# One filling block of a decoder layer moved from the RWKV-7 part to the HGRN2 stage, with the late half projections in other turns and the attention operands in fixed slots

## The chip, the cores and the metric

The kernel runs on one core of one Trainium2 chip. The metric is the device time of one execution in microseconds (us); lower is better. The kernel before took 1496.69 us, the median of three runs (1495.39 to 1498.95).

## The reference, cut to what matters

One decoder layer over 1024 tokens of width 1024, in float32. Three groups of heads work side by side on one input projection; a gated feed-forward with a short convolution, a gated embedding and a last normalization follow.

```
z = rmsnorm(h, norm_mix_g) @ w_in                  # 1024 x 3840
a_q, a_f, a_i, a_g, b_q, b_k, b_v, c_in = split(z)
o_a = hgrn2_mix(a_q, a_f, a_i, a_g, ...)           # 4 heads of 128, gated linear recurrence
o_b = dilated_window_mix(b_q, b_k, b_v)            # 4 heads of 64, three dilated windows
o_c = rwkv7_mix(c_in, ...)                         # 4 heads of 64, delta-rule recurrence
h = h + concat(o_a, o_b, o_c) @ w_out
h = h + conv_glu_ffn(rmsnorm(h), ...)
h = h + sigmoid(rmsnorm(h) @ w_g) * (p @ w_p)
return rmsnorm(h)
```

Sequence 1024, d_ff 2816. The change touches only how and when columns of `z` are computed and how the first two lines of heads use them; what is computed stays.

## The kernel before, in words

**Tiling.** All data lies transposed, channels on the 128 partitions and tokens along the free axis. `w_in` is cut into 30 column blocks of 128. A block is projected by 48 TensorE products of 128x128 by 128x512 (`mm3`, L125-L134): 8 row blocks, 2 halves of the tokens, and 3 products each, since every float32 operand is split into a high and a low part (`xh`, `xl` for the input, `whi`, `wlo` for the weights; `split2`, L102-L109, makes the weights' parts with a ScalarE cast and a subtraction on GpSimd or VectorE). Weights come through two buffers (`wraw`), the split parts through six of each kind (three blocks' worth).

**Stages.** First the norm of the input (`mix_norm`). Then RWKV (`rwkv`): blocks 0 to 7 are its own columns, done in two parts p = 0, 1 of two heads each. In each part there is a preparation, a small triangular inverse that runs on VectorE, and a main part (`rwkv_main`, `rwkv_groups`) of four groups of chunks, a chain of small products on TensorE with VectorE, ScalarE and GpSimd steps between them. The other 22 blocks (8 to 23 for HGRN2, 24 to 29 for attention) don't depend on RWKV, and are used as filling: while RWKV's chain waits for other engines, TensorE computes projections. A list in `rwkv` (L523) fixes their order, and `FILL = (6, 4, 6, 3)` says how many go to part 0's preparation, part 0's main part, part 1's preparation and part 1's main part. In a main part the filling is a generator of steps (`project_steps`): one step is three products, a block has 16, and `fill(k)` calls in `rwkv_groups` place k of them at given points: 11 in a group where the main part has four blocks (`more` = 1), 8 where it has three. A finished block is scaled, sometimes put through a sigmoid, and stored to device memory as `z` by the SP queue (`project_done`, L455).

**The HGRN2 stage** (`phase_mix`, L308-L328) starts when RWKV is through. Three blocks are then still missing. Four streams are interleaved in rounds by a string of letters: A is heads 0 and 2 of HGRN2, B heads 1 and 3 (from round 6), C the attention (`swa`, turns in `TURNS`), F the missing blocks (`project_late`, tiles `zp`), half a block (24 products) a turn, in rounds 1, 3, 5, 7, 9, 11, 13; its last turn frees the projection's input and makes the operand tiles of the output projection in its place. A turn of A or B is one step of a head (`hgrn_head`): load f and q of a head from `z` (SP queue, `zload`), make keys (`hk`) and gated queries (`qt`), scores (`hsc`), seven levels of a hierarchical product (`hsc` at L1023, with multiplications of `qt` and `hk` between them), transposes (`vt`), chunk states (`hkv`), outputs (`hpo`), their norm (VectorE, a power on GpSimd, VectorE), and a last transpose (`vt` at L1106) with the gate. Attention does two pairs of heads, eight query blocks each: scores (`swq`), a VectorE minimum, a ScalarE exponential, transposes (`swt`), values (`swo`). Its operands q, k, v and the turned V share four buffers of one tag, and the next pair's three are loaded together on GpSimd's queue after the last block of the first pair.

The letters give the priority only. A scheduler then writes each engine's instructions in the order in which its model expects them to become ready; each engine executes its list strictly in that order. In the main parts of RWKV the order is the program's own (`manual_schedule`).

**Pools.** Memory pools that are opened with `self.pool` wait for each tile's last user when memory is used again; those of `tc.tile_pool` (`hg`, `sw`, `rk0`, `rk1` before the change) wait for the whole pool.

After the stage `phase_out` multiplies by `w_out` (tiles `dp`), with the operands in the order 6, 7, 0, 1, 4, 2, 3, 5; its first products can fill the end of the HGRN2 stage.

Of the kernel before, what the change touches and what calls it, by code (L numbers as in the profile page):

```python
# [10 lines left out]
F32 = mybir.dt.float32  # L11
# [68 lines left out]
class Trunk:  # L80
# [227 lines left out]
    def phase_mix(self):  # L308
        nc, tc = self.nc, self.tc
        self.mix_norm()  # L310
        with tc.tile_pool(name="slots", bufs=1) as slots:
            self.slots, self.NSLOT = slots, 8
            self.rwkv()
        self.O, self.done = None, []
        for p in (0, 1):
            self.o_split(6 + p)
        with tc.tile_pool(name="hg", bufs=1) as slots, tc.tile_pool(name="sw", bufs=1) as sp:
            self.slots, self.NSLOT = slots, 11
            self.hgrn_setup()
            self.sp = sp  # L320
            self.swmask = sp.tile([P, T], F32, name="swmask")
            nc.scalar.dma_start(self.swmask, self.a["swm"])
            A = chain(self.hgrn_head(0), self.hgrn_head(2))
            B = chain(self.hgrn_head(1), self.hgrn_head(3))
            order = []
            for r in range(36):
                order += "C" * (r in self.TURNS) + "A" + "B" * (r > 5) + "F" * (r % 2 and r < 14)
            interleave(order, {"A": A, "B": B, "C": self.swa(sp), "F": self.project_late(self.rest)})  # L328

    TURNS = [i * 33 // 22 for i in range(23)]  # L330

    def mix_norm(self):

# [182 lines left out]
    def rwkv(self):  # L516
        nc, tc = self.nc, self.tc
        lt = self.mix_in(0, 6, "lora")
        nc.scalar.activation(lt[0:64, :], lt[0:64, :], AF.Tanh)
        sg = self.mix_in(1, 7, "sg")  # L520
        nc.scalar.activation(sg, sg, AF.Sigmoid)
        self.z = {}
        js = iter((*range(8, 16), 24, 25, 26, 16, 17, 18, 20, 21, 22, 27, 28, 29, 19, 23))  # L523
        for p in (0, 1):
            d = {}
            with tc.tile_pool(name=f"pre{p}", bufs=1) as tp:
                with tc.manual_schedule(engines={mybir.EngineType.PE}):
                    self.rwkv_prep(p, tp, lt, d, next(js))
                self.rwkv_inverse(p, tp, d)
            self.project_rest([next(js) for _ in range(self.FILL[2 * p] - 1)])  # L530
            E = mybir.EngineType
            self.pend = {}
            steps = self.project_steps([next(js) for _ in range(self.FILL[2 * p + 1])])
            with tc.tile_pool(name=f"rk{p}", bufs=1) as rp:
                with tc.manual_schedule(engines={E.PE, E.DVE, E.Activation, E.Pool}):
                    self.rwkv_main(p, rp, sg, d, steps)
                    for _ in range(2):
                        next(steps, None)
                    self.pending("w")
                    self.rwkv_norm_out(p, sg, d, 0)  # L540
            self.rwkv_norm_in(p, d, 1)
            for n in steps:
                self.pending("z")
            self.pending("z")
            self.rwkv_norm_out(p, sg, d, 1)
        self.rest = list(js)

    FILL = (6, 4, 6, 3)

    def rwkv_prep(self, p, tp, lt, d, j):  # L550

# [159 lines left out]
    def rwkv_main(self, p, rp, sg, d, steps):  # L711
        y = d["scf"]
        y3 = y.rearrange("p (c v) -> p c v", v=64)
        d.update(y=y, y3=y3)
        self.rwkv_groups(p, rp, d, y3, steps, 11 if self.FILL[2 * p + 1] > 3 else 8)

    def rwkv_norm_in(self, p, d, hf, parts=(0, 1, 2, 3)):

# [43 lines left out]
        if name in self.dbg:  # L762
            self.nc.sync.dma_start(self.dbg[name], t)

    def rwkv_groups(self, p, rp, d, y3, steps, n):

        nc, mxp = self.nc, self.mxp
        ar, v, gC = d["ar"], d["v"], d["gC"]
# [61 lines left out]
        quad("U", 0)  # L830
        nc.vector.memset(X, 0.0)
        nc.vector.memset(GM, 0.0)
        packed_rb(0)
        nc.gpsimd.memset(RB, 0.0)
        nc.gpsimd.memset(Kt, 0.0)
        for q in Q:
            for u in range(4):
                nc.vector.tensor_copy(add[q, u, 1, :], self.ident[q, q])
        add_ar(0)
        S, more = None, 1 if n > 8 else 0  # L840
        for g in range(4):
            cs, last = group(g), g == 3
            c2 = lambda b: slice(4 * g + 2 * b, 4 * g + 2 * b + 2)
# [104 lines left out]
            fill(more)  # L948


    def hgrn_setup(self):
# [19 lines left out]
    def hgrn_head(self, h):  # L971
# [127 lines left out]
        o3 = o.rearrange("p (c v) -> p c v", v=P)  # L1099
        nc.vector.tensor_tensor(o3, o3, rs.unsqueeze(2).broadcast_to([P, 8, P]), ALU.mult)  # L1100
        yield
        for hf in (0, 1):
            sl = slice((1 - hf) * HT, (2 - hf) * HT)
            pt = mxp.tile([P, HT], F32, tag="mx", name=self.nm("vt"))
            for c in range(4):
                nc.tensor.transpose(pt[:, c * P:(c + 1) * P], o3[:, hf * 4 + c, :], self.ident)  # L1106
            nc.vector.scalar_tensor_tensor(oa[:, sl], pt if hf else pt[:, ::-1], par[:, PC_GN + h:PC_GN + h + 1], oa[:, sl], ALU.mult, ALU.mult)
# [4 lines left out]

    def swa(self, sp):

        pend, fin, load = [], None, self.swa_load(sp, 0)
        yield
        for p in (0, 1):
            d = load
            self.swa_values_in(d)
# [17 lines left out]
    def swa_load(self, sp, p):  # L1137
        d = {"p": p}
        for i, n in enumerate("qkv"):
            d[n] = self.zload(24 + 3 * p + i, lambda n: sp.tile([P, T], F32, tag="sslot", name=self.nm(n), bufs=4),  # L1140
                              self.nc.gpsimd)
        return d

    def swa_values_in(self, d):
        nc, vc = self.nc, d["v"]
        V = self.sp.tile([P, T], F32, tag="sslot", name=self.nm("sV"), bufs=4)
# [706 lines left out]
```

## Time and profile before

| | us |
|---|---|
| median of three runs | 1496.69 |
| the profiled execution's own time | 1496.24 |
| its span, first to last instruction | 1494.5 |
| TensorE (PE) busy in the span | 1445.1 (97%) |
| VectorE (DVE) | 1097.8 (73%) |
| ScalarE (ACT) | 634.5 (42%) |
| GpSimd (POOL) | 446.6 (30%) |

In the trace, RWKV's first main part runs from 146.4 to 225.7 us, the second from about 349 to 421.6, and the HGRN2 stage from 433 to about 648. A view by windows gives the busy time of each engine within stretches of the span, and the clock that TensorE was granted (1.00 is full speed). A view of waits adds up, for an engine, the idle time in front of its instructions by what ended it. A timeline row has the start in us, the time from the first start to the last end of the merged instructions, engine, line, operation, tiles, and in brackets the idle time before it with its releaser. Products overlap in the array, so the distance between starts, not the length of one, is what a product costs. A float32 product stands twice in a row's count.

### The profile page before, as it was taken

The numbers are of one execution on the slowest core, as the hardware profiler recorded it, in microseconds if no ns is written. First come the engines' busy times: TensorE is split into PE (matmuls) and PEld (weight loads), VectorE is DVE, ScalarE is ACT, GpSimd is POOL, SyncE is SP. The second block draws the span as 40 slices with busy tenths as digits, with TensorE's granted clock in tenths as the row PEclk, the third lists the DMA queues.
The fourth block names the chain that finished last, engine by engine and source line by source line (L and its number), as shares of the span: only waits on it lengthen the run. The fifth ranks groups of instructions, "written<-read, shape, count | busy, mean of one in ns | idle before, by whom it ended". The sixth has DMA issues, their size and how long they took to land.

```text
span 1494.5 us, 20176 instructions
## 1 busy us (share of the span) xinstructions
PE 1445.1 (97%) x7416; PEld 1199.0 (80%) x7416; DVE 1097.8 (73%) x1650; ACT 634.5 (42%) x1121; POOL 446.6 (30%) x362
## 2 busy tenths in 40 slices
PE   8999999999989889999999999999999999999996
PEld 7888997888977677778878888888888888888775
DVE  7666455585648668736788888888888799777684
ACT  6531343213425635425454444444444444455542
POOL 3232432313412122112144554444554000002343
PEclk9999999999999989999999999999999999999998
DMA  6123112232152111165333333333332883351443
GB/s 219 58 92 99 43 56 72 72 99 63 43 179 74 42 73 57 43 229 194 127 110 98 103 106 106 106 106 106 106 106 81 313 298 97 105 164 42 139 157 106
DMA packets 79874, 167.83 MB, mean 112 GB/s; under 512 B 20064, under 2 KB 22240, under 8 KB 79776
## 3 DMA queue, kind: packets, MB, share of 16 engines
q1 hardware_dynamic: 65424, 145.44, 29.8%
q10 hardware_dynamic: 13264, 17.04, 3.4%
q0 software_dynamic: 1088, 4.06, 0.8%
q8 instruction: 58, 0.95, 0.3%
q14 instruction: 40, 0.33, 0.1%
HBM read 120.12 MB, written 46.40 MB: 111 GB/s over the span
## 4 chain that ended last, share of the span: by engine, by line
PE 84%; DVE 6%; issue 4%; POOL 2%; DMA 2%; ACT 1%; DVEq 0%; POOLq 0%; ACTq 0%; SPq 0%
PE bg L1325 16%; PE bv L1325 12%; PE dp L130 8%; PE dp L134 8%; PE dp L132 8%; PE bg L1626 7%; PE bv L1626 7%; PE hsc L1023 2%; DMA zl<-z 1%; PE swq L1167 1%; PE swo L1203 1%; POOL wlo L108 1%; PE bv L130 1%; PE bv L132 1%; PE swt L1190 1%
## 5 line engine op out<-in xcount | busy, mean ns | idle before, releaser
L130 PE MATMUL dp<-xh,whi 128*128 128x512 f32 x560 | 202.7, 406 | 1.1 <-ACT xh L374 1.1
L134 PE MATMUL dp<-xh,wlo 128*128 128x512 f32 x560 | 194.4, 391 | 2.0 <-POOL wlo L108 1.1
L132 PE MATMUL dp<-xl,whi 128*128 128x512 f32 x560 | 194.5, 391 | 0.4 <-DVE xl L375 0.3
L108 POOL TENSOR_TENSOR wlo<-raw,whi 128x512 fp32r<-128x512 f32 x84 | 138.0, 1662 | 77.8 <-ACT whi L106 77.8
L108 POOL TENSOR_TENSOR wlo<-wraw,whi 128x512 fp32r<-128x512 f32 x64 | 88.0, 1379 | 233.2 <-ACT whi L106 203.9
L1325 PE MATMUL bg<-t,whi 128*128 128x512 f32 x352 | 132.7, 389 | 0.0
L106 ACT CAST whi<-wraw 128x512 fp32r<-128x512 f32 x120 | 72.1, 617 | 132.7 <-PE dp L132 94.4
L134 PEld LDWEIGHTS dp<-xh,wlo 128*128 128x128 f32 x560 | 105.0, 188 | 25.0 <-POOL wlo L108 1.5
L130 PEld LDWEIGHTS dp<-xh,whi 128*128 128x128 f32 x560 | 104.5, 188 | 23.6 <-issue 3.8
L132 PEld LDWEIGHTS dp<-xl,whi 128*128 128x128 f32 x560 | 105.2, 188 | 21.8 <-DVE xl L375 1.4
L108 POOL TENSOR_TENSOR wlo<-s,whi 128x512 fp32r<-128x512 f32 x44 | 65.9, 1498 | 159.5 <-ACT whi L106 147.3
L1626 PE MATMUL bg<-t,whi 128*128 128x512 f32 x308 | 95.0, 389 | 0.0
L1626 PE MATMUL bv<-t,whi 128*128 128x512 f32 x308 | 94.8, 389 | 0.0
L106 ACT CAST whi<-raw 128x512 fp32r<-128x512 f32 x88 | 52.6, 619 | 97.4 <-PE bv L1325 49.0
L106 ACT CAST whi<-s 128x512 fp32r<-128x512 f32 x66 | 38.9, 620 | 120.7 <-PE bg L1325 113.3
L1325 PEld LDWEIGHTS bg<-t,whi 128*128 128x128 f32 x352 | 66.0, 188 | 13.6
L175 POOL TENSOR_TENSOR rst<-rst,mhalf 128x4 f32<-128x4 f32 (+1 forms) x9 | 9.8, 1088 | 223.4 <-DVE rst L173 223.4
L108 DVE TENSOR_TENSOR wlo<-wraw,whi 128x512 fp32r<-128x512 f32 x56 | 48.2, 863 | 34.8 <-ACT whi L106 32.4
L1622 ACT CAST t<-t 128x512 fp32r<-128x512 f32 x77 | 47.8, 622 | 47.8 <-PE bv L1626 34.8
L1626 PEld LDWEIGHTS bv<-t,whi 128*128 128x128 f32 x308 | 57.8, 188 | 12.1
L1626 PEld LDWEIGHTS bg<-t,whi 128*128 128x128 f32 x308 | 57.7, 188 | 12.0
L1325 PE MATMUL bg<-t,wlo 128*128 128x512 f32 x176 | 67.2, 389 | 0.0
(429 smaller groups left out, 3660.9 us busy)
## 6 DMA issues: line engine op xcount, KB each, us to landing
raw<-in_ffn_up_dram SPq DMA_DIRECT2D x44, 512.0 KB, 3.7
wraw<-in_w_in_dram SPq DMA_DIRECT2D x29, 512.0 KB, 3.6
z<-zst SPq DMA_DIRECT2D x19, 512.0 KB, 2.9
gb<-ct SPq DMA_DIRECT2D x33, 256.0 KB, 2.0
t<-gb SPq DMA_DIRECT2D x33, 256.0 KB, 2.8
t<-gt SPq DMA_DIRECT2D x33, 256.0 KB, 2.7
zl<-z SPq DMA_DIRECT2D x16, 512.0 KB, 3.5
wraw<-in_ple_gate_dram SPq DMA_DIRECT2D x16, 512.0 KB, 3.6
```

The costliest lines, as they stand in the source:

```text
L106: nc.scalar.copy(hi, src)
L108: eng.tensor_tensor(lo, src, hi.bitcast(F32), ALU.subtract)
L130: nc.tensor.matmul(ps[hf], wh, xh[hf], start=first, stop=False)
L132: nc.tensor.matmul(ps[hf], wh, xl[hf], start=False, stop=False)
L134: nc.tensor.matmul(ps[hf], wl, xh[hf], start=False, stop=last)
L1023: nc.tensor.matmul(sc[:, c, :], ks[:, c * P:(c + 1) * P], view(qt, c * P, [2 * n, 64 // n], [HT + n, 2], [1, n]), start=True, stop=True)
L1167: nc.tensor.matmul(pq[h][:, b:b + w], d["q"][hs, qb * P:nk], d["k"][hs, b:b + w], start=True, stop=True)
L1190: nc.tensor.transpose(pt[:, kb * P:(kb + 1) * P], lg[:, b + kb * P:b + (kb + 1) * P], self.ident)
L1203: nc.tensor.matmul(po[hs, :], d["V"][:, kb, hs], pT[h][:, kb * P:(kb + 1) * P], start=kb == 0, stop=kb == qb)
L1325: nc.tensor.matmul(ps, w[part == 2][:, s], X[k][part == 1], start=start and k == part == 0, stop=k == 3 and part == 2, skip_group_check=no ...
L1622: nc.scalar.copy(xh, x)
L1626: nc.tensor.matmul(ps[m], wt[part == 2][:, m * P:(m + 1) * P], (xh, xl)[part == 1], start=k == part == 0, stop=k == NK - 1 and part == 2)
```

## The change

`FILL` becomes (6, 3, 6, 3): part 0's main part has three filling blocks instead of four, and all later blocks move up by one, so that four blocks (28, 29, 19, 23) and not three (29, 19, 23) are left for the HGRN2 stage. `rwkv_groups` places 8 steps a group in both parts. F has turns in rounds 0, 1, 4, 7, 9, 11, 13, 15 and a last one in 17. A head's last turn comes one round later (a second `yield` before the final transposes). Attention's operands have a tag each; scores of the first block stand before the transposes of V; the next pair's k is loaded after block 5 (into the place of the first pair's v), its q and v after block 7, q on ScalarE's queue. The pools `hg`, `sw` and `rk` are opened with `self.pool`. At the start of `rwkv_groups`, memsets and copies that need no inverse stand before the two operations (`quad`) that read it.

```diff
-        with tc.tile_pool(name="hg", bufs=1) as slots, tc.tile_pool(name="sw", bufs=1) as sp:
+        with self.pool("hg") as slots, self.pool("sw") as sp:
...
-            for r in range(36):
-                order += "C" * (r in self.TURNS) + "A" + "B" * (r > 5) + "F" * (r % 2 and r < 14)
+            for r in range(38):
+                order += "C" * (r in self.TURNS) + "A" + "B" * (r > 5) + "F" * (r in self.LATE)
...
+    LATE = 0, 1, 4, 7, 9, 11, 13, 15, 17
...
-            with tc.tile_pool(name=f"rk{p}", bufs=1) as rp:
+            with self.pool(f"rk{p}") as rp:
...
-    FILL = (6, 4, 6, 3)
+    FILL = (6, 3, 6, 3)
...
-        quad("T", 0)
+        nc.vector.memset(X, 0.0)
+        nc.vector.memset(GM, 0.0)
...
+        quad("T", 0)
+        quad("U", 0)
         add_ar(0)
...
-            fill(1 + more)
+            fill(1)
...
-            fill(more)
...
         nc.vector.tensor_tensor(o3, o3, rs.unsqueeze(2).broadcast_to([P, 8, P]), ALU.mult)
         yield
+        yield
...
+        ds = {0: {"p": 0}, 1: {"p": 1}}
+        for n, tag in zip("qkv", ("sa", "sb", "sc")):
+            self.swa_load(ds[0], n, tag, nc.gpsimd)
...
                     cur = self.swa_scores(sp, d, qb)
+                if qb == p:
+                    self.swa_values_in(d)
...
-                if qb == 7 and p == 0:
-                    load = self.swa_load(sp, 1)
+                if p == 0 and qb == 5:
+                    self.swa_load(ds[1], "k", "sc", nc.gpsimd)
+                if p == 0 and qb == 7:
+                    self.swa_load(ds[1], "q", "sa", nc.scalar)
+                    self.swa_load(ds[1], "v", "sb", nc.gpsimd)
```

In the order of instructions the change shows at three places of the HGRN2 stage. The first is TensorE's list at the start of the stage: `yt` and `pg` end RWKV, `zp` is a late half projection, `swq` and `vt` are attention's first scores and the transposes of its V, `hsc` the first scores of HGRN2's head 0. Before:

```order
L755 MATMUL pg_3672<-sg_474,par 128x512
L1150 MATMUL vt_3705<-cst,zl_3698 128x128 x4
L1150 MATMUL vt_3711<-cst,zl_3698 128x128 x4
L1167 MATMUL swq_3718<-zl_3696,zl_3694 128x128
L1167 MATMUL swq_3719<-zl_3696,zl_3694 128x128
L130 MATMUL zp_3746<-xh_105,whi_3736 128x512
...
L134 MATMUL zp_3746<-xh_119,wlo_3738 128x512
L1167 MATMUL swq_3790<-zl_3696,zl_3694 128x256
L1167 MATMUL swq_3791<-zl_3696,zl_3694 128x256
L1002 MATMUL hsc_3776<-zl_3702,hk_3729 128x128 x4
```

And with the change:

```order
L756 MATMUL pg_3609<-sg_474,par 128x512
L130 MATMUL zp_3653<-xh_105,whi_3643 128x512
...
L134 MATMUL zp_3653<-xh_119,wlo_3649 128x512
L1171 MATMUL swq_3681<-zl_3633,zl_3631 128x128
L1171 MATMUL swq_3682<-zl_3633,zl_3631 128x128
L1154 MATMUL vt_3692<-cst,zl_3635 128x128 x4
L1154 MATMUL vt_3698<-cst,zl_3635 128x128 x4
L130 MATMUL zp_3710<-xh_89,whi_3643 128x512
...
L134 MATMUL zp_3710<-xh_103,wlo_3649 128x512
L1001 MATMUL hsc_3740<-zl_3639,hk_3705 128x128 x4
```

Two halves (48 products) instead of one now stand ahead of the first `hsc`; the scores of attention's second block moved behind it.

The second place is TensorE's list where attention passes from its first pair of heads to its second. `swt` are transposes of the first pair's exponentials; `swq` with the operands `zl_4396,zl_4394` (before) or `zl_4062,zl_4329` (now) are the second pair's first scores; `hpo` are outputs of HGRN2's head 0. Before:

```order
L1190 MATMUL swt_4383<-cst,lg_4211 128x128 x4
L1190 MATMUL swt_4389<-cst,lg_4211 128x128 x3
L1167 MATMUL swq_4629<-zl_4396,zl_4394 128x128
L1167 MATMUL swq_4630<-zl_4396,zl_4394 128x128
L1167 MATMUL swq_4712<-zl_4396,zl_4394 128x256
L1167 MATMUL swq_4713<-zl_4396,zl_4394 128x256
L1086 MATMUL hpo_4401<-hV_4250,hS_3773 128x128
```

With the change:

```order
L1106 MATMUL vt_4504<-cst,ho_4333 128x128 x4
L1022 MATMUL hsc_4514<-qt_3962,ks_4476 128x128 x4
L130 MATMUL zp_4525<-xh_89,whi_4429 128x512
...
L134 MATMUL zp_4525<-xh_103,wlo_4435 128x512
L189 MATMUL swd_4554<-cst,sden_3912 64x128 x8
L1171 MATMUL swq_4565<-zl_4062,zl_4329 128x128
L1171 MATMUL swq_4566<-zl_4062,zl_4329 128x128
```

The second pair's first scores moved from before head 0's outputs to behind them, behind the two last late halves and behind head 0's final transposes (`vt_4504`).

The third place is TensorE's list ahead of head 0's final transposes (`vt` from `ho`), which wait for the norm of the outputs. Before:

```order
L1190 MATMUL swt_4461<-cst,lg_4353 128x128 x4
L1190 MATMUL swt_4467<-cst,lg_4353 128x128 x4
L1023 MATMUL hsc_4483<-qt_4027,ks_4428 128x128 x4
L1106 MATMUL vt_4534<-cst,ho_4400 128x128 x4
L1106 MATMUL vt_4540<-cst,ho_4400 128x128 x4
```

With the change:

```order
L1022 MATMUL hsc_4416<-qt_3962,ks_4361 128x128 x4
L130 MATMUL zp_4439<-xh_105,whi_4429 128x512
...
L134 MATMUL zp_4439<-xh_119,wlo_4435 128x512
L1022 MATMUL hsc_4468<-qt_3962,ks_4424 128x128 x4
L1207 MATMUL swo_4479<-pT_4380,sV_3691 64x128
...
L1106 MATMUL vt_4498<-cst,ho_4333 128x128 x4
```

A late half, another level of head 1 and 16 products of attention's values moved in between.

More of the change, by code (lines that the diff above doesn't have):

```diff
@@ L714, in rwkv_main @@
         d.update(y=y, y3=y3)
-        self.rwkv_groups(p, rp, d, y3, steps, 11 if self.FILL[2 * p + 1] > 3 else 8)
+        self.rwkv_groups(p, rp, d, y3, steps)
     def rwkv_norm_in(self, p, d, hf, parts=(0, 1, 2, 3)):
@@ L763, in dump, with rwkv_groups @@
             self.nc.sync.dma_start(self.dbg[name], t)
-    def rwkv_groups(self, p, rp, d, y3, steps, n):
+    def rwkv_groups(self, p, rp, d, y3, steps):
         nc, mxp = self.nc, self.mxp
@@ L826, in rwkv_groups @@
         RB5, GM5 = (w.rearrange("p u (a h i) -> p u a h i", a=2, h=2) for w in (RB, GM))
-        quad("T", 0)
+        nc.vector.memset(X, 0.0)
+        nc.vector.memset(GM, 0.0)
+        for q in Q:
+            for u in range(4):
+                nc.vector.tensor_copy(add[q, u, 1, :], self.ident[q, q])
         scores_bd(0)
         keys_bd(0)
-        quad("U", 0)
-        nc.vector.memset(X, 0.0)
-        nc.vector.memset(GM, 0.0)
         packed_rb(0)
@@ L835, in rwkv_groups @@
         nc.gpsimd.memset(Kt, 0.0)
-        for q in Q:
-            for u in range(4):
-                nc.vector.tensor_copy(add[q, u, 1, :], self.ident[q, q])
+        quad("T", 0)
+        quad("U", 0)
         add_ar(0)
-        S, more = None, 1 if n > 8 else 0
+        S = None
         for g in range(4):
@@ L947, in rwkv_groups @@
                     nc.scalar.copy(y4[64 * c:64 * c + 64, 2 * g:2 * g + 2, h, :], py4[64 * h:64 * h + 64, :, c, :])
-            fill(more)
     def hgrn_setup(self):
@@ L1113, in swa @@
     def swa(self, sp):
-        pend, fin, load = [], None, self.swa_load(sp, 0)
+        nc, pend, fin = self.nc, [], None
+        ds = {0: {"p": 0}, 1: {"p": 1}}
+        for n, tag in zip("qkv", ("sa", "sb", "sc")):
+            self.swa_load(ds[0], n, tag, nc.gpsimd)
         yield
         for p in (0, 1):
-            d = load
-            self.swa_values_in(d)
+            d = ds[p]
             for qb in range(10):
@@ L1131, in swa, with swa_load @@
                     pend.append((qb, *cur))
-                if qb == 7 and p == 0:
-                    load = self.swa_load(sp, 1)
+                if p == 0 and qb == 5:
[3 more added lines that the diff above has]
+                    self.swa_load(ds[1], "v", "sb", nc.gpsimd)
                 yield
         self.swa_out(*fin)
[L1137 to L1142, printed above, removed]
+    def swa_load(self, d, n, tag, eng):
+        d[n] = self.zload(24 + 3 * d["p"] + "qkv".index(n),
+                          lambda nm: self.sp.tile([P, T], F32, tag=tag, name=self.nm(nm), bufs=1), eng)
     def swa_values_in(self, d):
         nc, vc = self.nc, d["v"]
-        V = self.sp.tile([P, T], F32, tag="sslot", name=self.nm("sV"), bufs=4)
+        V = self.sp.tile([P, T], F32, tag="sd", name=self.nm("sV"), bufs=1)
         for hf in (0, 1):
```

## The prediction

> **What bounds the kernel now.** I read the page first, then the stages by windows, then what TensorE waits for in the stage that shows gaps.
>
> ```profile
> span 1494.5 us, 20176 instructions
> PE 1445.1 (97%) x7416; PEld 1199.0 (80%) x7416; DVE 1097.8 (73%) x1650; ACT 634.5 (42%) x1121; POOL 446.6 (30%) x362
> PE   8999999999989889999999999999999999999996
> PEclk9999999999999989999999999999999999999998
> ```
>
> TensorE is the bound, 97% busy. The change adds and removes no product worth naming, so it can only win or lose what TensorE loses: idle time and slow clock. The slices show both between the 12th and 18th digit, 410 to 670 us. Windows narrow that down: the two main parts of RWKV, then the whole HGRN2 stage, then the four stretches in it with a clock below 1.00 and those between them.
>
> ```profile
> core 0: us, PE busy (x) PEld busy (x) DVE busy (x) ACT busy (x) POOL busy (x), PEclk, DMA share, GB/s
> 146.40:225.70 79.30, 78.95 (x553) 71.86 (x552) 42.18 (x91) 30.55 (x93) 29.83 (x36) 1.00 0.14 48
> 349.30:421.60 72.30, 70.96 (x513) 64.44 (x512) 41.68 (x89) 29.09 (x91) 28.79 (x35) 1.00 0.15 48
> 433.00:648.00 215.00, 190.43 (x1358) 153.54 (x1357) 150.57 (x289) 105.92 (x208) 46.25 (x39) 0.95 0.21 69
> 445.60:449.00 3.40, 3.40 (x18) 3.40 (x18) 1.95 (x5) 0.40 (x2) 0.21 (x1) 0.50 0.99 314
> 524.10:530.90 6.80, 5.54 (x24) 4.63 (x25) 1.05 (x6) 0.88 (x4) 0.00 (x0) 0.50 0.25 103
> 541.20:548.00 6.80, 5.49 (x34) 5.29 (x36) 5.68 (x8) 1.24 (x2) 1.82 (x3) 0.50 0.01 2
> 575.30:578.70 3.40, 3.37 (x18) 2.74 (x19) 3.30 (x6) 0.27 (x1) 0.00 (x0) 0.50 0.08 14
> ```
>
> RWKV's main parts have almost no gap (0.35 and 1.34 us). The HGRN2 stage has 215.00 - 190.43 = 24.6 us of idle TensorE. In four stretches the clock is half; TensorE is busy there for 3.40 + 5.54 + 5.49 + 3.37 = 17.8 us, which at full speed would be 8.9. So the stage loses 24.6 + 8.9 = 33.5 us. No other engine is near a bound: VectorE is busy 150.57 of 215. What TensorE waits for in the stage, in total, times, longest:
>
> ```profile
> PE vt L1106 <- DVE ho L1100: 8.0, 3, 4.4
> PE swq L1167 <- DMA zl<-z: 5.3, 1, 5.3
> PE hsc L1002 <- DVE hk L984: 3.7, 1, 3.7
> PE hsc L1023 <- DVE qt L1028: 3.4, 4, 1.6
> PE swt L1190 <- ACT ob L1204: 0.9, 1, 0.9
> ```
>
> Three rows hold 17.0 us. Their places in the timeline, with the idle time in brackets:
>
> ```profile
> 445.22 3.41 PE L1002 MATMUL hsc<-zl,hk 128*128 128x128 f32 x16 [3.72 <-DVE hk L984]
> 525.01 0.80 PE L1167 MATMUL swq<-zl,zl 64*128 64x128 f32 x4 [5.31 <-DMA zl<-z]
> 542.51 1.94 PE L1106 MATMUL vt<-cst,ho 128*128 128x128 f32 x8 [4.40 <-DVE ho L1100]
> 644.95 1.06 PE L1106 MATMUL vt<-cst,ho 128*128 128x128 f32 x8 [1.77 <-DVE ho L1100]
> ```
>
> The third wait of that group is 8.0 - 4.40 - 1.77 = 1.8 us, in front of head 1's `vt`. Each of the four slow stretches begins at the end of such a wait (445.6 after 445.22, 524.1 within the one that ends at 525.01, 541.2 within the one to 542.51; the fourth, at 575.3, is at head 1's). The same eight transposes take 1.94 us in the slow stretch and 1.06 outside. So a long wait is paid twice, and the wait of 1.77 that ends at 644.95 brought no slow stretch: the point lies near 1.8 us.
>
> The Trainium skill, TensorE: Matmul & The Clock Gate, section "Part 1: The HAM clock gate (the "warmup" mystery)", says that the array's clock falls to half after an idle window of about 3.4 us and returns after a busy one. The trace agrees with the half and with lengths of 3.40 and 6.80 us. By that rule the stretch after the 1.8 us wait has another cause and stays, 3.37 / 2 = 1.7 us less to win, and the sum below would be 1477.1; the trace puts it right behind a wait, and I follow the trace.
>
> **The change part by part.**
>
> *RWKV's first main part.* The price of a block: a late half is 24 products, and the first and last of one start at
>
> ```profile
> 435.14 0.50 PE L130 MATMUL zp<-xh,whi 128*128 128x512 f32 x1
> 440.48 0.39 PE L134 MATMUL zp<-xh,wlo 128*128 128x512 f32 x1
> ```
>
> so 5.34 / 23 = 0.232 us each, 5.6 a half and 11.1 a block. Part 1 already runs with three blocks and 8 steps a group; it is the row to go by. Part 0 shortens from 79.30 to about 72.30, 7.0 us; four steps fewer remain behind the groups (16 x 4 - 44 - 2 = 18 before, 48 - 32 - 2 = 14 after), 12 products or 2.8 us. That is 9.8 of 11.1: thinner filling costs **+1.3**. Bounds: 0.3 (part 0's gap stays as it is) and 2.6 (twice it). The memsets ahead of `quad` and the pools' finer waits work where TensorE has a gap of 0.35 us in all: nothing to win, and no wait added.
>
> *Start of the stage.* TensorE waits for keys that need head 0's f. SP's queue had been held:
>
> ```profile
> 419.17 15.57 SPq L97 DMA_DIRECT2D wraw<-in_w_out_dram  x2
> 434.80 0.42 SPq L464 DMA_DIRECT2D z<-zst  x1
> 435.38 1.73 SPq L502 DMA_DIRECT2D zl<-z  x2
> 443.04 0.81 DVE L981 TENSOR_SCALAR zl<-zl,olb,lb 128x1024 f32<-128x1024 f32 x1 [6.70 <-DMA zl<-z]
> ```
>
> Two prefetches of `w_out` wait there for weight buffers, then come the last block's store and f's load, which lands 7.7 us later. With the change one prefetch, the store and the loads stand there in the same order, and the prefetch waits for a split that the last filling block's end releases, as now; so I leave f's landing where it is, and the wait is hidden, not shortened: a second half, 5.6 us, stands in front of `hsc`, against 3.72 of wait. **-3.7**. Bounds: 0 (f later by the difference and more) and -3.7. A new wait: GpSimd's load of the next pair's k now waits for both stores of block 28, and behind it in that queue stands head 0's third key multiplication. The second half ends near 446 (440.48 and one half more), its store a few us later, and the multiplication stands now at
>
> ```profile
> 454.90 1.16 POOL L1026 TENSOR_TENSOR hk<-hk,hT 128x512 f32<-128x512 f32 x1
> ```
>
> so I take 0, up to 3 if the store is late.
>
> *The change of pairs.* Before, GpSimd issues the second pair's last loads at
>
> ```profile
> 518.30 1.12 POOL L502 DMA_DIRECT2D zl<-z  x2
> ```
>
> and TensorE's list has the scores that need them ahead of head 0's ready outputs. Now outputs, levels, two halves and the values of two blocks stand between; the two halves alone are 11.1 us, against a landing of 525.01 - 518.30 = 6.7. **-5.3**; it can't cost more than now, and 0 only if the q load were issued over 4.4 us after the first of those halves began. Its issue on ScalarE's queue, some 0.4 us like SP's, is off the path.
>
> *Final transposes of a head.* For head 0 a half (5.6), a level and 16 value products now stand in between, against 4.40; for head 1 a round with two levels and attention. Head 3 is last, has only `dp` products behind it, and keeps its 1.77. **-6.2** (8.0 - 1.8), bounds -8.0 and -3.
>
> *Slow clock.* All four stretches followed waits that go. **-8.9**, bounds 0 and -8.9.
>
> *The added block.* Its 11.1 us are TensorE's in both places, counted above. On VectorE it brings two scalings of 0.68 (below) into a stage where VectorE has 64 us free; nothing on the path.
>
> *The end.* Head 3's steps come two rounds later, but attention still ends in round 33. Before, the values of attention's last block and `swd` covered head 3's transposes and states:
>
> ```profile
> 627.91 1.97 PE L1203 MATMUL swo<-pT,sV 128*64 128x128 f32 x32
> 631.70 1.09 PE L189 MATMUL swd<-cst,sden 128*64 128x128 f32 x16
> 443.77 0.68 DVE L469 TENSOR_TENSOR zst<-zp,rstd 128x512 f32<-128x512 f32 x1
> ```
>
> In the new list `swo` is gone from there, and `swd` stands ahead of the transposes. So up to 1.97 + 1.09 = 3.1 us of cover are lost, 0 at best; **+2.0**, nearer to the upper end, since both copies to the states' operands follow the transposes.
>
> Sum: +1.3 - 3.7 - 5.3 - 6.2 - 8.9 + 2.0 = -20.8, against the profiled execution's own 1496.24 (0.45 under the median): **1475.4 us**. Some 0.2%, 3 us, is what a measurement of this kernel can tell from no change.
>
> **Rivals.**
>
> *All of it.* The short waits (24.6 - 17.0 = 7.6, 3.4 of them for `qt`) go too, since halves are spread over more rounds, and the end costs nothing: 1496.24 - 24.6 - 8.9 + 1.3 = 1464.0. Against: rounds after 17 have no filling. 10%.
>
> *Waits change place.* TensorE runs ahead of VectorE and ScalarE, and half of the long waits return, with half of the slow clock: 1496.24 - 7.6 - 4.5 + 1.3 + 2.0 = 1487.4. For: two levels with only a little attention between them have a gap today,
>
> ```profile
> 461.95 1.13 PE L1023 MATMUL hsc<-qt,ks 128*128 128x128 f32 x8 [1.65 <-DVE qt L1028]
> ```
>
> and the new list has that shape at the start of the stage too; the scheduler's model misjudged a load once already. Against: the new long stretches without a half are few. 16%.
>
> *Slower.* The stage is not TensorE's but the chain of heads 1 and 3: from round 6 on. Then halves in rounds 13 and 15, formerly absent, lie in that chain, its products wait behind them, and the gaps stay: +1.3, +2.0, and two scalings of 0.68 on VectorE in the chain, 1.4: 1496.24 + 4.7 = 1500.9. It decides if a head's round needs longer than the work that TensorE has for a round. Against: TensorE's waits for `qt` sum to 3.4 us in four cases. 6%, with what falls between it and no change.
>
> That the moved block isn't in the stage can't be: the list shows it.
>
> **How the numbers follow.** Forecast 68%, its own range 1470 to 1481 from the bounds of the start and the end. With 10% at 1464, 16% at 1487 and 6% at 1500, the range from 1466 to 1487 leaves out about a fifth. Faster: 68 + 10 + 14 = 92%; same 3%; slower 5%.
>
> **What would show it.** Right: no wait over 1.8 us between 430 and 640 us, no row of the stage with a clock of 0.50, no `swq` wait for a DMA; the first main part near 72 us; the stage some 11 us shorter than 215 in spite of the added 11.1 (-3.7 - 5.3 - 6.2 - 8.9 + 2.0 + 11.1); one `vt` wait of about 1.8 at the end. Wrong: slow clock after new waits on `qt` or `lg`; f landing later than 11 us after the last filling product; gaps of more than 2.6 us in the first main part.

## The result, and the profile after

The changed kernel took 1486.25 us, the median of four runs (1483.15 to 1486.52), beside 1497.7 us for the kernel before in the same set. The ratio is 0.9919, with a 95% interval from 0.9903 to 0.9936. So it is faster by about 11.5 us, a little more than half of the 20.8 that the sum gave. The profiled execution took 1486.12 us, 10.1 less than the one of before. Its span is 10.2 us shorter (1494.5 to 1484.3); the steps below are accounted against these 10.2.

The page's lines of the changed kernel that answer to those of before, span, busy time and TensorE's two rows of slices:

```profile
span 1484.3 us, 20168 instructions
PE 1447.7 (98%) x7416; PEld 1197.7 (81%) x7416; DVE 1096.2 (74%) x1652; ACT 631.7 (43%) x1119; POOL 448.5 (30%) x360
PE   9999999999999999989999999999999999999997
PEclk9999999999999999999999999999999999999998
```

The hole between the 12th and 18th slice is nearly closed. The view by windows, with the columns as in the prediction, shows RWKV's two main parts, the HGRN2 stage and the output projection behind it (up to the first product into `bv`; some products of the gated embedding already lie in it):

```profile
146.80:218.70 71.90, 70.74 (x514) 64.35 (x513) 43.00 (x90) 30.15 (x92) 28.72 (x35) 1.00 0.13 43
341.30:415.40 74.10, 71.32 (x513) 64.22 (x512) 40.90 (x90) 30.20 (x93) 28.80 (x36) 1.00 0.13 39
426.80:635.60 208.80, 197.78 (x1409) 157.86 (x1409) 153.54 (x292) 103.83 (x208) 50.65 (x39) 0.99 0.21 74
635.60:735.60 100.00, 97.05 (x423) 78.92 (x422) 56.49 (x85) 38.98 (x64) 20.23 (x16) 0.97 0.57 198
```

The output projection was not shown before; its stretch in the kernel before is this row of the same view:

```profile
648.00:743.50 95.50, 94.50 (x427) 77.71 (x427) 57.17 (x85) 38.92 (x64) 19.26 (x16) 1.00 0.57 201
```

The stage went from 215.0 to 208.8 us although it took in a block, and TensorE's idle time in it from 24.6 to 11.0. But RWKV's second main part grew from 72.3 to 74.1, and the output projection from 95.5 to 100.0 with a clock of 0.97. What TensorE waits for within the stage now, in total, times, longest:

```profile
PE hsc L1022 <- DVE qt L1027: 3.9, 4, 1.7
PE vt L1106 <- DVE ho L1099: 1.7, 1, 1.7
PE hpo L1085 <- ACT ob L1208: 1.1, 1, 1.1
```

The three long waits of before are gone. The longest wait of this part of the program now lies behind the stage, in the timeline at

```profile
655.31 0.50 PE L130 MATMUL dp<-xh,whi 128*128 128x512 f32 x1 [2.32 <-ACT whi L106]
```

and it is followed by 6.8 us of half clock.

### The profile page after: what moved, and what is told of

Read it like the earlier page. It is cut to its first block, busy times and chain, and to the rows that moved or that the text cites. A ratio compares the mean times of both kernels' runs of the same rounds, so it can differ in the third digit from the quotient of the medians.

```text
span 1484.3 us, 20168 instructions
## 1 busy us (share of the span) xinstructions
PE 1447.7 (98%) x7416; PEld 1197.7 (81%) x7416; DVE 1096.2 (74%) x1652; ACT 631.7 (43%) x1119; POOL 448.5 (30%) x360
## 5 line engine op out<-in xcount | busy, mean ns | idle before, releaser
L130 PE MATMUL dp<-xh,whi 128*128 128x512 f32 x544 | 198.6, 409 | 3.7 <-ACT whi L106 2.3
L134 PE MATMUL dp<-xh,wlo 128*128 128x512 f32 x544 | 189.8, 394 | 0.5 <-POOL wlo L108 0.5
L132 PE MATMUL dp<-xl,whi 128*128 128x512 f32 x544 | 189.7, 393 | 0.1
L175 POOL TENSOR_TENSOR rst<-rst,mhalf 128x4 f32<-128x4 f32 (+1 forms) x9 | 10.2, 1135 | 222.3 <-DVE rst L173 222.3
L1329 PEld LDWEIGHTS bg<-t,whi 128*128 128x128 f32 x352 | 66.1, 188 | 13.6
```

The costliest lines, as they stand in the source:

```text
L130: nc.tensor.matmul(ps[hf], wh, xh[hf], start=first, stop=False)
L132: nc.tensor.matmul(ps[hf], wh, xl[hf], start=False, stop=False)
L134: nc.tensor.matmul(ps[hf], wl, xh[hf], start=False, stop=last)
L175: nc.gpsimd.tensor_tensor(r2[:, :n], r[:, :n], self.mhalf[:, :n], ALU.pow)
L1329: nc.tensor.matmul(ps, w[part == 2][:, s], X[k][part == 1], start=start and k == part == 0, stop=k == 3 and part == 2, skip_group_check=no ...
```

## The experiments

The time of one kernel varies by 3 to 10 us between executions, in most kernels more through the granted clock than otherwise. So two more numbers stand beside each median, means over all timed runs of a kernel: the span times its granted clock (the time that it would take at full speed), and the rest of the span (what the slow clock cost). The clock is given to three digits, so the split of a single run is uncertain by 0.7 us; the time at full speed itself scatters by up to 1.9 us (standard deviation) among the four to twelve executions of a kernel, so differences of about 1 us between two rows are not told apart.

| kernel | median us | ratio to before (95%) | at full speed | slow clock |
|---|---|---|---|---|
| before, beside the experiments (3 sets) | 1496.0 to 1497.9 | | 1477.0 to 1478.6 | 18.1 to 18.6 |
| changed | 1486.25 | 0.9919 (0.9903 to 0.9936) | 1472.2 | 11.5 |
| move alone | 1488.46 | 0.9942 (0.9926 to 0.9958) | 1473.3 | 13.1 |
| operands alone | 1490.22 | 0.9947 (0.9932 to 0.9961) | 1473.1 | 15.4 |
| second yield alone | 1503.56 | 1.0038 (1.0024 to 1.0052) | 1479.2 | 22.8 |
| changed, move undone | 1490.18 | 0.9952 (0.9936 to 0.9968) | 1473.8 | 14.1 |
| changed, old turns | 1489.69 | 0.9948 (0.9934 to 0.9962) | 1475.3 | 13.2 |
| changed, old operands | 1497.0 | 0.9998 (0.9982 to 1.0014) | 1477.6 | 17.8 |
| changed, no second yield | 1477.12 | 0.9872 (0.9853 to 0.9890) | 1469.3 | 6.6 |
| changed, other list | 1483.01 | 0.9905 (0.9887 to 0.9923) | 1469.6 | 11.4 |
| changed, sums later | 1485.41 | 0.9925 (0.9907 to 0.9943) | 1473.0 | 10.6 |
| changed, casts first | 1481.65 | 0.9896 (0.9877 to 0.9914) | 1471.4 | 8.1 |
| changed, other list, casts first | 1478.88 | 0.9875 (0.9853 to 0.9896) | 1469.2 | 7.8 |
| changed, other list, no second yield | 1478.81 | 0.9870 (0.9853 to 0.9887) | 1465.9 | 10.9 |

### Two losses outside the stage

**The list.** Since all blocks move up by one, RWKV's second main part gets blocks 21, 22, 27 instead of 22, 27, 28. Block 21 goes through a sigmoid on ScalarE (`zst<-dp`). In the changed kernel, TensorE's timeline and then ScalarE's in the third group of that part:

```profile
381.08 1.16 PE L878 MATMUL pu<-U,Y 128*128 128x128 f32 x8 [0.79 <-ACT Y L858]
...
384.91 1.10 PE L891 MATMUL pk<-vt,AKt 128*128 128x64 f32 x8 [0.62 <-ACT kt L824]
```

```profile
377.87 0.60 ACT L473 ACTIVATE zst<-dp 128x512 f32<-128x512 f32 x1
379.96 0.60 ACT L473 ACTIVATE zst<-dp 128x512 f32<-128x512 f32 x1 [1.49 <-DVE dp L306]
380.45 0.58 ACT L858 COPY Y<-py 128x512 f32<-128x512 f32 x1
```

The second sigmoid, which itself waits for VectorE, stands ahead of the copy `Y` that the chain needs; TensorE's idle time in this part is 74.10 - 71.32 = 2.8 us against 1.34 before. The experiment exchanges block 21 for a plain one:

```diff
-        js = iter((*range(8, 16), 24, 25, 26, 16, 17, 18, 20, 21, 22, 27, 28, 29, 19, 23))
+        js = iter((*range(8, 16), 24, 25, 26, 16, 17, 20, 21, 18, 22, 27, 28, 29, 19, 23))
```

> The changed kernel with block 18 in the place of block 21 in the list of filling blocks (20, 21, 18, 22 instead of 18, 20, 21, 22), so that part 1's main part gets three blocks without a sigmoid. Theory: the two sigmoids of block 21 on ScalarE stand ahead of the copy Y and cost TensorE 2.1 us of waits in group 2 of part 1; they go, and part 1's main part gets near 72.3 us from 74.1: 1483 to 1485 us. Rival, the thinner filling itself is what costs RWKV its saving: part 1 keeps its length, and the time stays at 1486 us.

It took 1483.01 us, 2.7 less at full speed, with the slow clock's share unchanged. The windows of the two traces agree:

```profile
341.00:412.40 71.40, 70.70 (x513) 64.38 (x512) 41.79 (x90) 29.05 (x91) 29.11 (x36) 1.00 0.13 40
```

The part takes 71.4 us instead of 74.1, and has 0.7 us idle. The rival, that thinner filling itself costs the saving, falls for this part.

**The output projection: first theory.** In the changed kernel VectorE waits for the raw weights of the feed-forward, and h's additions stand behind that:

```profile
646.72 0.69 DVE L1437 TENSOR_TENSOR s<-raw,raw 128x512 f32<-128x512 f32 x1 [6.24 <-DMA raw<-in_ffn_up_dram]
```

The experiment queues those sums behind the addition of h's row 4:

```diff
+                if m == 4 and g == 0:
+                    self.add4 = add.ins
...
-            sums(d)
+            with self.tc.issue_after(self.add4) if f == 0 else nullcontext():
+                sums(d)
```

> The changed kernel with one edit in the order of VectorE: the first unit's sums of ffn_up's raw weights stand behind h's addition of row 4 and not ahead of h's first additions. Theory: VectorE's wait of 6.2 us for the raw weights holds h's additions, the norm behind them, ScalarE's casts and so TensorE's product dp (2.3 us of wait and 3.4 us of slow clock); with the sums later these go, 1480 to 1483 us. Rival, the burst of loads is itself the cause (h's rows and the weights come at once and late): VectorE then waits for h instead, and the time stays at 1485 to 1487 us.

It took 1485.41 us, which can't be told from the changed kernel, and TensorE's wait in front of `dp` stayed at 2.32 us. That theory fell. So did its rival's picture: in this trace VectorE's addition of row 1 waits 7.1 us for TensorE's products and not for a load.

**Second theory.** ScalarE's timeline of the changed kernel at that place, the square of h's row 2 (`sqt`) among the casts of the next row's weights (`whi`):

```profile
651.63 0.60 ACT L106 CAST whi<-wraw 128x512 fp32r<-128x512 f32 x1
653.74 0.33 ACTq L1249 DMA_DIRECT2D hd<-h  x1
654.12 0.63 ACT L200 ACTIVATE sqt<-h 128x512 f32<-128x512 f32 x1 [1.88 <-DVE h L1248]
654.65 1.64 ACT L106 CAST whi<-wraw 128x512 fp32r<-128x512 f32 x3
```

And the same place before:

```profile
662.92 1.65 ACT L106 CAST whi<-wraw 128x512 fp32r<-128x512 f32 x3
666.85 0.33 ACTq L1245 DMA_DIRECT2D hd<-h  x1
667.22 0.63 ACT L200 ACTIVATE sqt<-h 128x512 f32<-128x512 f32 x1 [2.66 <-DVE h L1244]
```

Three casts came first before, one does now. That closes a loop: TensorE ends row 2, VectorE adds, ScalarE stores and squares, and only then casts the second half of row 3's weights, for which TensorE waits. The experiment makes row 3's casts ahead of row 2's store and square:

```diff
+            w = ahead and self.load_w(self.a["w_out"][ahead])
...
-                nc.scalar.dma_start(self.hd[m][g], u)
+                with self.tc.issue_after(self.cast) if ahead else nullcontext():
+                    nc.scalar.dma_start(self.hd[m][g], u)
...
-            self.sq_acc(acc, self.h[m][:, :HT], m == 0)
+            with self.tc.issue_after(self.cast) if m == 2 else nullcontext():
+                self.sq_acc(acc, self.h[m][:, :HT], m == 0)
```

> The changed kernel with one edit in ScalarE's order behind the stage: the store and the square of h's row 2 stand behind both casts of w_out's row 3, where the changed kernel has them behind the first cast alone. Theory: TensorE's wait of 2.3 us for the second half of row 3's weights is a loop (last product of row 2, addition, store, square, cast, next product) that this order closes; with the cast ahead the wait and its slow clock (3.4 us) go, 1480 to 1483 us. Rival, the burst of loads or the weights' own landing holds the cast: the wait stays with another releaser, 1485 to 1487 us.

It took 1481.65 us, 4.6 less. Its trace has the two casts ahead, and TensorE's waits there are shorter:

```profile
651.38 0.50 PE L130 MATMUL dp<-xh,whi 128*128 128x512 f32 x1 [0.42 <-ACT whi L106]
653.37 0.79 PE L134 MATMUL dp<-xh,wlo 128*128 128x512 f32 x1 [1.26 <-DVE wlo L108]
```

2.32 + 0.54 became 0.42 + 1.26. So the order of the casts is shown as the cause of the wait. Of what it cost, the table puts 0.8 us at full speed, which is within the scatter, and 3.4 us in slow clock. Both corrections together:

> The changed kernel with both corrections, block 18 in the place of block 21 in the list and the casts of w_out's row 3 ahead of row 2's store and square. If the two costs are separate places of the program, they add: 3.2 us for the list as measured and 4 to 5 for the casts, 1477 to 1480 us. Rival, a wait removed at the one place only moves to the next: 1482 to 1484 us.

1478.88 us, 3.0 us less at full speed than the changed kernel and 3.7 less of slow clock: separate places, which add.

### The parts of the change

**The second yield.** Which edit turned ScalarE's order, some 20 us behind the end of the stage? In the scheduler's order the three casts come first again as soon as the second `yield` is taken out, and only one comes first when it is put alone into the kernel before.

```diff
         nc.vector.tensor_tensor(o3, o3, rs.unsqueeze(2).broadcast_to([P, 8, P]), ALU.mult)
         yield
-        yield
```

> The changed kernel without the second yield, so that a head's final transposes come one turn earlier. In the scheduler's list this also restores three casts ahead of row 2's square behind the stage. Theory: the waits of the final transposes return in the stage (3 to 6 us with 1.7 us or more of slow clock) and the loss behind the stage goes (4.6 us), so 1485 to 1489 us. Rival, the new turns cover the transposes without the yield: 1481 to 1483 us, and the yield is what costs.

Both theories missed: 1477.12 us, 9 us faster than the changed kernel. By windows, its stage and its output projection:

```profile
426.20:632.40 206.20, 193.60 (x1406) 155.05 (x1405) 155.12 (x292) 106.48 (x210) 47.87 (x39) 1.00 0.22 77
632.40:726.90 94.50, 94.36 (x427) 77.69 (x426) 56.81 (x85) 38.69 (x65) 20.02 (x16) 1.00 0.60 204
```

The output projection is 5.5 us shorter than the changed kernel's and has 0.14 us idle, and the stage is 2.6 shorter too. The waits of the stage in the same kernel:

```profile
PE vt L1105 <- DVE ho L1099: 3.6, 2, 1.8
PE hsc L1022 <- DVE qt L1027: 2.3, 4, 0.8
PE swo L1206 <- DVE zl L1106: 2.1, 1, 2.1
```

Head 0's wait of 4.4 us does not come back without the yield; two of 1.8 and one of 2.1 stand in the place of the changed kernel's three of 1.6 to 1.7 (`qt` twice, `vt` once). So head 0 is covered without the yield, by the added late halves (the move alone, below, has no wait there either), and the yield exchanges waits. Put alone into the kernel before (with two more rounds), it shows that plainly:

```diff
         yield
+        yield
```

> The kernel before with nothing but the second yield ahead of a head's final transposes. Theory of the forecast: the waits of head 0 and head 1 (6.2 us) go with their slow clock (5.1 us), the end costs 2.0: 1487 to 1490 us. Rival from the runs so far: the yield puts ScalarE's row 2 ahead of the second cast behind the stage here too, so that 4.6 us are lost there, and heads with less filling around them gain little: 1493 to 1499 us.

1503.56 us, slower than before. TensorE's waits in it:

```profile
PE hsc L1023 <- DVE qt L1028: 12.0, 6, 5.6
PE hsc L1002 <- DVE hk L984: 4.9, 2, 4.1
PE swq L1168 <- DMA zl<-z: 4.0, 1, 4.0
PE vt L1107 <- DVE ho L1100: 1.7, 1, 1.7
```

`vt` fell from 8.0 to 1.7 us, as the forecast's step says, and `qt` rose from 3.4 to 12.0. VectorE's timeline shows why:

```profile
541.08 2.07 DVE L1100 TENSOR_TENSOR ho<-ho,hrs 128x1024 f32<-128x1024 f32 x1 [1.56 <-POOL hrs L1098]
543.07 0.71 DVE L1025 COPY_PREDICATED hS<-cmask,hsc 128x512 f32<-128x512 uint8 x1
543.68 0.67 DVE L1028 TENSOR_TENSOR qt<-qt,hT 128x512 f32<-128x512 f32 x1
```

Head 1's next `qt` is queued behind head 0's norm, which waits for GpSimd. Whichever product TensorE has next here, transposes or scores, waits for the same stretch of VectorE. What removed the wait in these runs was more work on TensorE in between.

**The move alone**, in the kernel before:

```diff
-    FILL = (6, 4, 6, 3)
+    FILL = (6, 3, 6, 3)
...
-                order += "C" * (r in self.TURNS) + "A" + "B" * (r > 5) + "F" * (r % 2 and r < 14)
+                order += "C" * (r in self.TURNS) + "A" + "B" * (r > 5) + "F" * (r % 2 and r < 18)
```

> The kernel before with nothing but the move: one filling block leaves RWKV's first main part and joins the HGRN2 stage, with the old turns (odd rounds up to 17) and the old attention operands. Theory of the forecast: RWKV's parts get about 7 us shorter in all, the added block's 11.1 us lie in the stage, and nothing else removes the waits for attention's q (5.3 us) and for the heads' ready outputs (4.4 and 1.8), so 1494 to 1500 us. Rival, the move itself is what fills the waits: two more halves in rounds 15 and 17 and a later start are enough, 1486 to 1490 us.

1488.46 us: the rival is right. Two more halves in rounds 15 and 17, with all other turns in the old places, make up about two thirds of the whole gain. Two waits in its trace:

```profile
PE vt L1106 <- DVE ho L1100: 4.7, 2, 3.0
PE swq L1167 <- DMA zl<-z: 2.0, 1, 2.0
```

The stage is only 1.7 us longer than before with 11.5 us more of products, since head 0's wait is gone and the one for q has fallen from 5.3 to 2.0 us, although head 1's grew from 1.8 to 3.0. The opposite, the changed kernel with the block back in RWKV (`FILL = (6, 4, 6, 3)`, `LATE = 0, 1, 4, 7, 9, 11, 13`):

> The changed kernel without the move: four filling blocks in RWKV's first main part with 11 steps a group as before, three late blocks in rounds 0, 1, 4, 7, 9, 11 and 13; the new pools, attention operands and second yield stay. If the turns and the operands carry the gain, the stage loses its long waits with seven halves too and the list of part 1 stays 22, 27, 28, so 1484 to 1489 us. Rival, the gain needs the added work as cover (two halves fewer in rounds 15 and 17, where heads 1 and 3 wait): 1491 us or more.

1490.18 us, near the rival. The waits for q and f stay away, but one of 5.2 us for `qt` stands in the stage, where the two missing halves had been:

```profile
PE hsc L1024 <- DVE qt L1029: 9.1, 5, 5.2
```

**The turns.** The changed kernel with `LATE = 1, 3, 5, 7, 9, 11, 13, 15, 17`:

> The changed kernel with the late halves in the odd rounds 1 to 17, as before, instead of 0, 1, 4, 7 and the odd rounds 9 to 17. Theory of the forecast: the second half ahead of the first scores is what covers f's landing, so the wait at the stage's start returns (2.1 to 3.7 us with 1.7 us of slow clock), 1489 to 1492 us. Rival, the stage already starts earlier and f with it, and the order of the first halves is worth nothing: 1485 to 1487 us.

1489.69 us, as the forecast's theory has it: 3.1 us more at full speed and 1.7 of slow clock. Its first `hsc` waits again:

```profile
437.41 0.79 PE L1001 MATMUL hsc<-zl,hk 128*128 128x128 f32 x5 [2.19 <-DVE hk L983]
```

**The operands**, alone in the kernel before, by the change's own lines in `swa`, `swa_load` and `swa_values_in`:

> The kernel before with nothing but the attention operands in fixed places (second pair's k loaded two steps earlier, q issued by ScalarE, the values transposed one step later). Theory of the forecast: TensorE's wait for q (5.3 us) goes with the slow clock behind it (3.4 us), 1488 to 1491 us. Rival, the operands help only with the new turns around them, and with the old ones another wait stands at the change of pairs: 1494 to 1498 us.

1490.22 us, and no wait for a DMA in front of `swq`: the forecast's theory. But q is not all that the operands change. In the same trace VectorE's first step on f starts at 439.65 us, 3.4 us earlier than before, with the stage starting at the same place, and the start's wait of 3.7 us is nearly gone:

```profile
PE hsc L1002 <- DVE hk L984: 0.6, 1, 0.6
```

So how much of the gain is q's and how much f's was not separated. Undone in the changed kernel:

> The changed kernel with the attention operands of before (four shared buffers, all three loads of the second pair at its last score step). Theory: TensorE waits for the second pair's q again, 2 to 5.3 us, with 1.7 to 3.4 us of slow clock, 1489 to 1494 us. Rival, the new turns alone put enough work ahead of the scores that need q: 1485 to 1487 us, no wait for a DMA.

1497.0 us, no faster than the kernel before at all; more than any theory gave. Its stage has these waits:

```profile
PE hsc L1022 <- DVE qt L1027: 6.3, 4, 3.3
PE hsc L1022 <- ACT pT L1191: 2.3, 1, 2.3
PE swq L1167 <- DMA zl<-z: 2.2, 1, 2.2
```

Only the last was foreseen. Why the others appear with this combination was not isolated.

**The fastest.** The other list and no second yield:

> The changed kernel without the second yield and with block 18 in the place of block 21 in the list. If the list's cost in RWKV and the yield's cost behind the stage are separate, they add: 1477.1 less 3.2, 1472.5 to 1475.5 us, the fastest of all. Rival, the earlier stage only moves a wait behind it: 1476 to 1478 us.

1478.81 us by the median, ratio 0.9870, not to be told from the kernel without the yield (0.9872). At full speed it is 3.4 us faster, as the list's correction should make it, and in the profiled execution RWKV's second part has its 2.8 us back; but the slow clock cost 10.9 us on average instead of 6.6. Whether that difference is the kernel's or that of so few executions (four and five) stays open.

The pools and the order of the memsets ahead of `quad` were not tried by themselves.

## Why the prediction was right, and where not

The sign, the range and the account of the stage's idle time held; the time came out 10.9 us above the number, near the upper end. It lies outside the forecast's own range, 1470 to 1481 us. Only the wider range, which was stretched to take in the rival "Waits change place", holds it, and that rival's mechanism is not what happened; to that extent the range held by luck. Two of the signs named for a right forecast failed: one row of the stage has a clock of 0.50 (509.00 to 512.40 us), and the stage is 6.2 us shorter, not 11. By its own steps, against the spans of the profiled executions:

| step | forecast | found |
|---|---|---|
| RWKV's first main part and what follows it | -9.8 | -9.0 |
| RWKV's second part | 0 | +2.8 |
| idle time of the stage (start, pairs, heads, end) | -13.2 | -13.6 |
| slow clock of the stage | -8.9 | -7.2 |
| products of the stage beside the slow clock | +11.1 | +14.6 |
| output projection | 0 | +4.5 |
| feed-forward and later | 0 | -2.3 |
| sum | -20.8 | -10.2 |

**RWKV, +1.3.** By the starts of `yt`, the first main part ends 7.0 us earlier and the stretch behind it is 2.0 shorter (12.9 to 10.9), so the step held within its bounds, 0.8 us short. It failed by what it left out. "Part 1 already runs with three blocks and 8 steps a group; it is the row to go by" compares numbers of blocks, and leaves out which blocks part 1 would now get. By the same starts, part 1 grew from 183.1 to 185.9 us, and with the other list it took 183.1.

**Start, -3.7.** The wait of 3.72 us is gone; the first `hsc` follows the second half without idle time. The old turns bring 2.19 of it back, so the second half in front is worth about 2.2; the other 1.5 came from f, which the step had left "where it is". It landed earlier: VectorE's first step on it

```profile
435.08 0.81 DVE L980 TENSOR_SCALAR zl<-zl,olb,lb 128x1024 f32<-128x1024 f32 x1 [0.72 <-DMA zl<-z]
```

comes 8.0 us before that of the kernel before, while the stage starts 6.2 us earlier.

**Change of pairs, -5.3.** Right: no wait for a DMA is left, and the operands alone do it. A wait of 1.09 us for `ob` stands near the place.

**Final transposes, -6.2.** The total at `vt` fell by 6.3, from 8.0 to 1.7 by the view of waits, so the number held. The reason held for head 0 alone: the added halves cover it, without the second yield too. For head 1 the wait only moved, from `vt` (1.80 us without the yield) to `qt` (1.60 with it), and the yield costs 9 us in this kernel.

**Slow clock, -8.9.** The stretches of before went, as forecast, and one of 3.4 us came (1.7 lost). Over all runs the slow clock fell from about 18.3 to 11.5 us, 6.8 less, with the new stretch behind the stage included.

**The end, +2.0.** Not found: the last `vt` waits 1.72 us against 1.77. The end did cost, but behind the stage.

**Products.** Full-speed busy time in the stage should have been 190.43 - 8.9 + 11.1 = 192.6 us; it is 197.78 - 1.7 = 196.1. The added block cost 11.5 by the starts of its products, 0.4 more. Without the yield the stage's busy time is 193.60, so 2.5 of the rest go with the yield; most of that lies in `swq`, whose 96 products take 27.6 us by their starts, against 25.6 without the yield and 25.3 before (at full speed). Why they take longer stays open: in the move alone, which has no second yield, they take 27.2.

**Output projection, 0.** The step that failed most: the text ends the change at the stage, and takes for granted that the scheduler writes the same order behind it. It did not; the casts' experiment gives 4.6 us back.

**Feed-forward and later, 0.** Of the 2.3 us, 1.6 are a wait of TensorE for `acc` that the trace of before has and that of the changed kernel has not; why it went stays open.

Of the rivals, "Waits change place" names the time that came (1487.4), by another mechanism: the long waits of the stage did not return, and the cost lies in RWKV's second part, in the yield and behind the stage. Its mechanism exists all the same: it is what the yield alone does (12.0 us at `qt`), and what is left when the block is not moved (5.2 at `qt`). "Slower" and "All of it" were not seen. Undoing any one of the parts that help loses 3.4 to 10.8 us. A part is not worth the same alone and in the changed kernel (move 7.5 and 3.9, operands 7.7 and 10.8, yield -5.6 and -9.1, by medians), so the gains do not simply add.

## What to carry to other kernels

When an element leaves an ordered list, ask of every later stage which elements it now gets and what else they need than the engine that they fill. A turn that comes later can change the order that a scheduler writes beyond the stage: compare the in-order queues of all engines behind the edit, and look for a cast or a copy that now stands behind something that waits for its own consumer. Split times into the part at full speed and the part lost to the clock before comparing runs; here 3.4 us that hide in the medians of two kernels (1477.1 and 1478.8) show at full speed (1469.3 and 1465.9).

## What the runs showed of the hardware

Between the start-up and the end of these executions the slow clock comes in stretches that are multiples of 3.41 us (3.41, 6.83, once 10.24) on a fixed grid, whose position differs from execution to execution. Whether a cell of that grid turns slow goes with TensorE's busy time in the cell before it. Four pairs of cells, the first two of the changed kernel, then one of the kernel before and one with the casts first (TensorE's busy time in the first of a pair, the clock in the second):

```profile
505.60:509.00 3.40, 1.63 (x12) 1.34 (x13) 1.72 (x6) 3.39 (x8) 0.00 (x0) 1.00 0.97 368
509.00:512.40 3.40, 3.40 (x18) 3.40 (x18) 0.00 (x0) 0.90 (x2) 0.00 (x0) 0.50 0.75 298
...
652.40:655.80 3.40, 1.08 (x5) 0.46 (x3) 2.49 (x4) 1.69 (x4) 0.47 (x1) 0.99 0.95 364
655.80:659.20 3.40, 2.86 (x8) 2.02 (x7) 0.87 (x1) 0.49 (x1) 2.54 (x2) 0.50 0.45 128
```

```profile
459.30:462.70 3.40, 1.75 (x11) 0.95 (x10) 3.40 (x7) 1.82 (x6) 0.00 (x0) 1.00 0.52 163
462.70:466.10 3.40, 3.40 (x18) 2.85 (x17) 3.31 (x8) 1.90 (x5) 0.27 (x1) 1.00 0.00 0
```

```profile
506.60:510.00 3.40, 2.31 (x21) 2.08 (x19) 0.62 (x2) 2.24 (x5) 0.00 (x0) 1.00 1.03 406
510.00:513.40 3.40, 3.40 (x41) 3.28 (x42) 0.93 (x2) 2.38 (x4) 0.00 (x0) 1.00 0.52 194
```

The first pair and the last hold the same two waits (0.69 and 1.09 us). In the changed kernel's execution both lie in one cell, TensorE is busy 1.63 us of it, and the next cell runs at half clock; with the casts first the grid divides them, and it costs nothing. Over the 14 traces of this case, of the cells at full clock (from 20 us to 15 us before the end) all 28 with TensorE busy under 45% were followed by a slow one, 15 of 49 between 45 and 60%, and none of 74 between 60 and 76%. The least idle of the cells that a slow one followed had TensorE idle for 1.40 us (in the kernel with the other list). So idle time of some 1.4 us or more can be paid a second time, but only when that much of it falls into one cell, and the point "near 1.8 us", as the prediction read it from one execution, is rather a chance that grows with the wait.

The Trainium skill, TensorE: Matmul & The Clock Gate, section "Part 1: The HAM clock gate (the "warmup" mystery)", says that the window is 3413 ns long and runs freely, without regard to the start of a kernel. The trace agrees, with 3.41 us and a grid that shifts between executions. It also says that the clock falls after an idle window; here a window in which TensorE is busy up to some 45% is enough, 1.08 of 3.40 us in the row at 652.40 above, and the one at 505.60 was enough with 1.63. The forecast weighed that rule as a reason for the fourth slow stretch of before to stay; it went.
